# One decoder step on one core: a pool of 52 slots of 576 columns in place of 53 of 568, and another order of the last operations

## The chip, the core and the metric

The kernel runs on one core of a Trainium2 chip. A core has five engines with instruction streams of their own: TensorE (PE in the profile; its weight loads are listed apart as PEld), VectorE (DVE), ScalarE (ACT), GpSimd (POOL) and SyncE (SP), which here only issues transfers. They work on SBUF, a memory of 128 partitions, and TensorE writes its products to PSUM banks of 128 x 512 fp32. Sixteen DMA engines move data between DRAM and SBUF. [...] The metric is the time of one execution on the device, in microseconds, lower being better.

## The reference

A decoder layer is run once for two groups of tokens: a prompt of 512 and 8 samples of 4, together 544 tokens of 1,024 features, all in fp32.

```python
h = rmsnorm(x, norm_mix_pre);  x_r, q, k, v, g = split(h @ w_in)
A = rg_lru(causal_conv4(x_r))                  # gated linear recurrence
B = window_attention(q, k, v)                  # 8 heads, 2 kv heads, window 128, sinks, bias
m = (sigmoid(g_A) * (A @ w_lru_o) + sigmoid(g_B) * (B @ w_attn_o)) @ w_out
x = x + rmsnorm(m, norm_mix_post)
u = causal_conv3(rmsnorm(x, norm_ffn_pre) @ w_up)       # 1024 -> 8192 columns
val, gate = split(u)
x = x + rmsnorm((gelu(gate) * val) @ w_down, norm_ffn_post)   # 4096 -> 1024
```

Returned are `x` of both groups and the states that a next step needs: the end of the recurrence, the last rows ahead of each convolution (among them `s_ffn_conv`, the last two rows of `u` per sample), and the last keys and values.

## The kernel before

**Number format.** Every large product is made of three: weight and activation are each split into a high part of reduced precision and a low rest, and `wh*xh`, `wh*xl` and `wl*xh` are summed in PSUM (`mm`, L165; `product`, L1531). ScalarE makes the high part of a weight by a copy and VectorE the low part by a subtraction (L168). The tokens stand along the columns in two halves, 272 each in the up projection, 256 and 288 in the down projection (`HALF`). A matmul has a weight block of 128 x 128 and a moving operand, the high or low part of an activation tile, of 256 to 288 columns.

**Stages.** In-projection, recurrence, attention, their two projections and the out-projection come first; the feed-forward part starts near 500 us. The up projection handles 32 pairs of a value block and a gate block. A pair is made of seven products of half size instead of eight (`pair`, L1644): `a11`, `a12`, `p2`, `p3`, `p1`, `p4`, `a22`, on the activation tiles `b11`, `b21`, `t2`, `t3`, `t1`, `b22`, `t4` (high parts end in H, low parts in L). They go to PSUM banks called `pux`, `puy` and `puz`. The weights of `p2` and `p4` are sums of blocks that the DMA engines add up in place (`raw_up_s`, L1468 and L1469; those of the last pair are loaded plainly at L1435). After a pair come the convolution taps and the gated product: `z` is the product, `fH` its high part (ScalarE) and `fL = z - fH` (VectorE, L168). Four such blocks make a chunk of the down projection, whose results (`pmdn`) VectorE adds to `ft`, the sum for each of the eight feature blocks (L174). The last chunk is called `dl`.

**Order.** TensorE's order is a table (`plan`) that interleaves the products of up and down projection. One entry is a slot: `slot()` runs what was put down for it (`result`, `later`), splits weights four entries ahead (`consumed`, `ahead`) and lets side jobs go on (`start_at`). The code of the feed-forward part runs under a manual schedule for ScalarE and VectorE, so that these execute in the order in which the code issues; the transfers of SP fall under it from L1987 on, and are placed by the scheduler before. A side job that matters here is `ffn_states` (L1765): three times it transposes a group of state rows into a slot, `ffn_rows_s`, and GpSimd issues four stores of it to DRAM (L1773). The second is started three slots after the `a22` of pair 27.

**Pools.** Most large tiles are slots of one pool, `S`, of 53 buffers of 128 x 568 fp32 (L144): the activation parts, `fH` and `fL`, `ft`, `ffn_rows_s`, the last `raw_up_s` halves, and the last weights. A few tiles of the same width stand outside of the pool. A new tile gets the buffer of a tile that is done with; the first instruction that writes the new tile then waits for the last ones that used the old. A column is 4 bytes, so that a slot is 2,272 bytes per partition. Smaller tiles (`T`, `RAW`, weight parts) come from pools of their own, and `pvn` is a small table of 24 columns with norm weights.

**The end.** Two of the four tiles of 128 prompt tokens are computed with tokens along the partitions (`tokens`, L1921; the last quarter in `ends`, L1952). `tokens_done` (L1932) adds the sum so far (`fr`), has ScalarE square it, and multiplies by the norm's weights (`fg`, the gain): on GpSimd for the first half of the first tile (L1943), else on VectorE (L171). `rstd` makes the tile's norm factor, and `tokens_out` (L1974) applies it, adds `x` in one operation (`stt`, L177) and returns the store of 256 KB. The other tokens, feature-major, are finished by `finish_b` (L1827): per block an `stt` on VectorE and an addition on GpSimd (L1837); `y_blocks` (L1852) then transposes pieces into `yb_p`, which leaves in sixteen small stores on SP (L1866), and into `yb_s`, the samples, which leave in four stores on GpSimd (L1850). `rows_t` (L1870) makes the rest of them on TensorE (`yo`).

Of the kernel before, what the change touches and what calls it, by code (L numbers as in the profile page):

```python
# [11 lines left out]
F32 = mybir.dt.float32  # L12
F32R = mybir.dt.float32r
AF = mybir.ActivationFunctionType
ALU = mybir.AluOpType
AX = mybir.AxisListType

P = 128
# [21 lines left out]
SCALE = HD ** -0.5  # L40
SKEY = 2 * WIN + NKV * NS

S_BUFS = 53
W_BUFS = 12
T_BUFS = 10
RAW_BUFS = 5
SLOT = 568
CH = 4
CHAIN = 10
AHEAD = 4  # L50
# [73 lines left out]
def hawk_step(ctx, tc, I, O):  # L124
    nc = tc.nc
    act, dve, pool, pe = nc.scalar, nc.vector, nc.gpsimd, nc.tensor

    keep = ctx.enter_context(tc.tile_pool(name="const", bufs=1))
    sp = ctx.enter_context(tc.tile_pool(name="slots", bufs=S_BUFS))
    wp = ctx.enter_context(tc.tile_pool(name="wsplit", bufs=W_BUFS))  # L130
# [12 lines left out]
    def S(name, dt=F32):  # L143
        return sp.tile([P, SLOT], dt, tag="s", name=name)  # L144

    def T(name, dt=F32):
        return tp.tile([P, FLAT + 4], dt, tag="t", name=name)

    def RAW(name):
        return rp.tile([P, D], F32, tag="raw", name=name)  # L150

    def PM(name):
        return psm.tile([P, 512], F32, tag="mm", name=name)
# [4 lines left out]
    def SM(name, shape, tag="sm"):  # L158
        return smp.tile(shape, F32, tag=tag, name=name)

    def f32(ap):
        return ap.bitcast(F32)

    def mm(out, l, r, start, stop):
        pe.matmul(out, l, r, start=start, stop=stop)  # L165

    def sub(out, a, b):
        dve.tensor_tensor(out=out, in0=a, in1=b, op=ALU.subtract)  # L168

    def mul(out, a, b):  # L170
        dve.tensor_tensor(out=out, in0=a, in1=b, op=ALU.mult)  # L171

    def add(out, a, b):
        dve.tensor_tensor(out=out, in0=a, in1=b, op=ALU.add)  # L174

    def stt(out, a, s_, b, op0, op1):
        dve.scalar_tensor_tensor(out=out, in0=a, scalar=s_, in1=b, op0=op0, op1=op1)  # L177
# [117 lines left out]
    class Full:  # L295
# [5 lines left out]
        def alloc(self, k):  # L301
            new = S if k or self.name not in APART else (lambda nm, dt: cp.tile([P, SLOT], dt, name=nm))
            self.t[k] = (new(f"{self.name}H{k}", F32R), new(f"{self.name}L{k}", F32R))
            return self.t[k]
# [95 lines left out]
    for r, nme in ((8, "norm_mix_post"), (16, "norm_ffn_pre"), (24, "norm_ffn_post")):  # L400
        nc.sync.dma_start(out=rows_a[r:r + 8, :], in_=I[nme].rearrange("o (k p) -> (o k) p", p=P))
    pv = keep.tile([P, 96], F32, name="pv")
    pvn = keep.tile([P, 24], F32, name="pvn")

    pw = PM("ps_warm")
    ps0 = PX("ps_rows_a0")
# [11 lines left out]
    def newton_rstd(r, v, s_, sq):  # L418

        act.activation(r, sq, AF.Abs_reciprocal_sqrt, scale=1.0 / D, bias=epst)  # L420
        dve.tensor_scalar(v, sq, 1.0 / D, EPS, ALU.mult, ALU.add)
        mul(s_, r, r)
        stt(s_, s_, -0.5, v, ALU.mult, ALU.mult)
        stt(r, s_, 1.5, r, ALU.add, ALU.mult)
# [552 lines left out]
    def gates(c):  # L977
        xH, xL = T(f"xcH{c}", F32R), T(f"xcL{c}", F32R)
        act.activation(xH[:, 0:FLAT], xc[c][:, 0:FLAT], AF.Copy)
        sub(xL[:, 0:FLAT], xc[c][:, 0:FLAT], f32(xH[:, 0:FLAT]))  # L980
        rg[c] = cp.tile([P, SLOT], F32, name=f"rg{c}") if c < RG_APART else S(f"rg{c}")
        yield
# [612 lines left out]
    def slot(k=1, lag=1, limit=10 ** 6, chain_first=False):  # L1595

        for f in todo.pop(turn[0], []):
            f()
        if k and not chain_first:
            consumed(k, lag, limit)  # L1600
        turn[0] += 1
        round_()
        if k and chain_first:
            consumed(k, lag, limit)
# [157 lines left out]
    def by_block(ap):  # L1762
        return ap.rearrange("p (c a d) -> p c a d", a=4, d=32)
# [38 lines left out]
    for i, x in enumerate(plan):  # L1802
# [8 lines left out]
        else:  # L1811
            _, q, c, a = x
# [28 lines left out]
                    if z >= 0:  # L1841
                        y_blocks(z)

    yb = {}

    def samples_out():
        src = yb["s"][:, 0:256].rearrange("p (c d) -> p c d", c=8)
# [4 lines left out]
    def y_blocks(c):  # L1852

        if c == 0:
            yb["p"], yb["s"] = T("yb_p"), T("yb_s")
        dve.transpose(yb["s"][:, 32 * c:32 * c + 32], ft[c][:, SEQ:NT])
        if c > 3:
            return
        o = yb["p"][:, 0:512].rearrange("p (b c d) -> p c b d", b=4, c=4)
        dve.transpose(o[:, c], ft[c][:, 2 * P:3 * P].rearrange("p (b q) -> p b q", b=4))  # L1860
        if c == 3:
            dst = yp[2 * P:3 * P, 0:512].rearrange("(b q) (c a d) -> a b q c d", b=4, a=4, d=32)
            src = yb["p"][:, 0:512].rearrange("p (b c d) -> p b c d", b=4, c=4)
            for a in range(4):
                for b in range(4):
                    nc.sync.dma_start(out=dst[a, b], in_=src[32 * a:32 * a + 32, b])  # L1866

    yo_ = {}

# [40 lines left out]
    def turned():  # L1910
        px = PX("pfo")
        for j in range(4):
            pe.transpose(px[:, j * P:(j + 1) * P], ft[4 + j][:, 0:P], ident)
        row = T("frow0_1")[:, 0:512]
        frow[0, 1] = by_block(row)
        later(1, act.copy, row, px)
# [4 lines left out]
    def tokens(i, kk):  # L1921
        ps = PM(f"ptok{i}_{kk}")
        t = slice(i * P, (i + 1) * P)
        for k in range(CH):
            wh, wl = (usplit["dl", k, kk][j].rearrange("p k n -> p (k n)") for j in range(2))
            fh, fl = (F.t[QL * CH + k][j][:, t] for j in range(2))
            mm(ps, fh, wh, k == 0, False)
            mm(ps, fl, wh, False, False)
            mm(ps, fh, wl, False, k == CH - 1)
        return ps  # L1930

    def tokens_done(i, kk, ps):  # L1932

        fr = T(f"fr{i}_{kk}")[:, 0:512]
        add(by_block(fr), frow[i, kk], by_block(ps[:, 0:512]))
        jk = T(f"jk{i}_{kk}")[:, 0:512]
        act.activation(jk, fr, AF.Square, accum_out=ssq[:, i, kk:kk + 1])
        fg = fgs[i, kk] = T(f"fg{i}_{kk}")[:, 0:512]
        g = gpost[:, kk * 512:(kk + 1) * 512]
        if i or kk:  # L1940
            mul(fg, fr, g)
        else:
            pool.tensor_tensor(out=fg, in0=fr, in1=g, op=ALU.mult)  # L1943

    def rstd(i):
        add(ssq[:, i, 0:1], ssq[:, i, 0:1], ssq[:, i, 1:2])
        st = SM(f"nst_t{i}", [P, 3], "nst_t")
        v, r, s_ = (st[:, z:z + 1] for z in range(3))
        newton_rstd(r, v, s_, ssq[:, i, 0:1])
        return r  # L1950
# [23 lines left out]
    def tokens_out(i, r, z):  # L1974
        o = fgs[i, z]
        stt(o, o, r, xtok[i, z], ALU.mult, ALU.add)
        return lambda: nc.sync.dma_start(out=yp[i * P:(i + 1) * P, z * 512:(z + 1) * 512], in_=o)

    acc = T("acc31")
    gpost = RAW("gpost")  # L1980
# [15 lines left out]
    for _, q, c, a in held:  # L1996
        down(q, c, a, down_done(q, c))
        slot(0)
    for i, kk in ((0, 0), (0, 1), (1, 0)):
        ps = tokens(i, kk)  # L2000
        if (i, kk) == (0, 0):
            slot(0)
            turned()
        slot(0)
        tokens_done(i, kk, ps)
        if (i, kk) == (0, 1):
            r0 = rstd(0)
    while todo or side:
        slot(0)
    samples_out()  # L2010
    outs = [tokens_out(0, r0, z) for z in range(2)]
    for f in outs:
        f()
    fgs[1, 1] = T("fg1_1")[:, 0:512]
    st = SM("nst_t1", [P, 5], "nst_t1")
    v, r, s_, b_, h_ = (st[:, z:z + 1] for z in range(5))
# [53 lines left out]
```

## Time and profile before

| | |
|---|---|
| time, median of 3 runs | 971.44 us (970.93 to 971.70) |
| the profiled execution's own time | 971.33 us |
| its span in the trace | 969.5 us |
| mean granted clock of TensorE | 0.998 of full speed |
| instructions | 20,081 |
| TensorE busy | 99% of the span, 7,598 matmuls |
| VectorE, ScalarE, GpSimd busy | 79%, 57%, 17% |
| read from and written to DRAM | 118.21 MB and 16.74 MB |

The trace covers the span; the 1.8 us between span and time lie around it. Rows of a group give the line of the code, the engine, the operation, `out<-in` with the shape, the count, and behind the bar the busy time in microseconds and the mean of one in nanoseconds; a row of a timeline gives the start and the duration in microseconds. In the table by windows the columns are the stretch and its length, the busy time (and number) of PE, PEld, DVE, ACT and POOL, the granted clock, the share of the time in which the DMA engines had work, and GB/s. "SPq" or "POOLq" is the queue in which an engine waits to issue a transfer. In a list of waits each row names who waited, for what, and the sum, number and longest of the waits.

### The profile page before, as it was taken

The numbers are of one execution on the slowest core, as the hardware profiler recorded it, in microseconds if no ns is written. First come the engines' busy times: TensorE is split into PE (matmuls) and PEld (weight loads), VectorE is DVE, ScalarE is ACT, GpSimd is POOL, SyncE is SP. The second block draws the span as 40 slices with busy tenths as digits, with TensorE's granted clock in tenths as the row PEclk, the third lists the DMA queues.
The fourth block names the chain that finished last, engine by engine and source line by source line (L and its number), as shares of the span: only waits on it lengthen the run. The fifth ranks groups of instructions, "written<-read, shape, count | busy, mean of one in ns | idle before, by whom it ended". The sixth has DMA issues, their size and how long they took to land.

```text
span 969.5 us, 20081 instructions
## 1 busy us (share of the span) xinstructions
PE 959.9 (99%) x7598; PEld 952.4 (98%) x7598; DVE 762.1 (79%) x1625; ACT 550.2 (57%) x1342; POOL 168.5 (17%) x284
## 2 busy tenths in 40 slices
PE   9999999999999999999999999999999999999997
PEld 8999999999999999999999999999999999999996
DVE  5778888857858555689967878887888888888886
ACT  6544443467476425566867665555556565656642
POOL 2142000003406231230011110101011111111024
PEclk9999999999999999999999999999999999999999
DMA  7765536533334537235147575767667685859542
GB/s 226 237 212 185 148 90 155 158 94 88 93 103 152 172 101 197 66 123 178 46 108 196 133 187 141 182 155 170 167 153 196 142 201 134 204 130 234 178 147 93
DMA packets 247596, 147.26 MB, mean 152 GB/s; under 512 B 36324, under 2 KB 231788, under 8 KB 247468
## 3 DMA queue, kind: packets, MB, share of 16 engines
q1 hardware_dynamic: 237468, 124.15, 43.5%
q0 software_dynamic: 9824, 19.55, 11.9%
q10 hardware_dynamic: 208, 2.30, 0.6%
q8 instruction: 59, 0.97, 0.4%
q14 instruction: 37, 0.30, 0.1%
HBM read 118.21 MB, written 16.74 MB: 139 GB/s over the span
## 4 chain that ended last, share of the span: by engine, by line
PE 91%; DVE 5%; ACT 1%; issue 1%; SPq 1%; DMA 1%; DVEq 0%; POOL 0%; ACTq 0%; POOLq 0%
PE pmin L165 20%; PE pmdn L165 17%; PE pux L1531 16%; PE puy L1531 8%; PE pq L1531 6%; PE pmlo L165 5%; PE pmao L165 5%; PE pmout L165 4%; PE puz L1531 4%; PE pg L165 1%; PE pvp L165 1%; PE psc L165 1%; SPq L1866 1%; DVE wl_e L168 1%; DMA pt<-pd 0%
## 5 line engine op out<-in xcount | busy, mean ns | idle before, releaser
L165 PE MATMUL pmin<-hH,wh_in 128*128 128x256 f32 (+1 forms) x568 | 163.9, 291 | 0.0
L165 PE MATMUL pmin<-hL,wh_in 128*128 128x256 f32 (+1 forms) x568 | 162.4, 288 | 0.0
L165 PE MATMUL pmin<-hH,wl_in 128*128 128x256 f32 (+1 forms) x568 | 159.1, 288 | 0.0
L165 PE MATMUL pmdn<-fH,wh_dn 128*128 128x256 f32 (+1 forms) x448 | 129.2, 288 | 0.0
L165 PE MATMUL pmdn<-fH,wl_dn 128*128 128x256 f32 (+1 forms) x448 | 128.8, 287 | 0.0
L165 PE MATMUL pmdn<-fL,wh_dn 128*128 128x256 f32 (+1 forms) x448 | 128.7, 287 | 0.0
L165 PEld LDWEIGHTS pmin<-hH,wh_in 128*128 128x128 f32 x568 | 107.2, 189 | 1.4 <-issue 1.2
L165 PEld LDWEIGHTS pmin<-hL,wh_in 128*128 128x128 f32 x568 | 107.2, 189 | 0.1
L165 PEld LDWEIGHTS pmin<-hH,wl_in 128*128 128x128 f32 x568 | 104.7, 188 | 0.2 <-issue 0.2
L177 DVE SCALAR_TENSOR_TENSOR uc<-u,fv,uc 128x560 f32<-128x560 f32 x128 | 102.0, 797 | 1.7 <-ACT uc L1562 1.2
L165 PEld LDWEIGHTS pmdn<-fH,wl_dn 128*128 128x128 f32 x448 | 84.4, 188 | 0.0
L165 PEld LDWEIGHTS pmdn<-fL,wh_dn 128*128 128x128 f32 x448 | 84.3, 188 | 0.1
L165 PEld LDWEIGHTS pmdn<-fH,wh_dn 128*128 128x128 f32 x448 | 84.2, 188 | 0.1
L1659 ACT COPY u<-pux 128x272 f32<-128x272 f32 x52 | 20.1, 387 | 87.2 <-PE pux L1531 87.2
L168 DVE TENSOR_TENSOR u<-puy,u 128x240 f32<-128x240 f32 (+2 forms) x78 | 24.6, 344 | 48.1 <-PE puy L1531 30.5
L174 DVE TENSOR_TENSOR ft<-ft,pmdn 128x256 f32<-128x256 f32 (+1 forms) x104 | 45.0, 434 | 16.5 <-PE pmdn L165 16.3
L283 ACT ACTIVATE wh_in<-raw_in 128x512 fp32r<-128x512 f32 x70 | 42.2, 624 | 19.2 <-issue 12.0
L290 DVE TENSOR_TENSOR wl_in<-raw_in,wh_in 128x512 fp32r<-128x512 f32 x70 | 47.8, 693 | 1.0 <-ACT wh_in L283 1.0
L1562 ACT ACTIVATE uc<-u,fv 128x560 f32<-128x560 f32 x64 | 48.2, 756 | 0.0
L781 ACT ACTIVATE s<-s,st 128x256 f32<-128x256 f32 (+1 forms) x32 | 15.2, 475 | 53.6 <-DVE st L778 45.9
L168 DVE TENSOR_TENSOR wl_dn<-raw_dn,wh_dn 128x512 fp32r<-128x512 f32 x56 | 38.3, 684 | 3.1 <-ACT wh_dn L1480 3.1
L1469 POOL DMA_DIRECT2D raw_up_s<-raw_up_s x26 | 22.4, 861 | 92.2 <-DMA raw_up_s<-raw_up__11280 5.4
(746 smaller groups left out, 3371.9 us busy)
## 6 DMA issues: line engine op xcount, KB each, us to landing
raw_in<-in_w_in_dram SPq DMA_DIRECT2D x35, 512.0 KB
raw_dn<-in_w_down_dram SPq DMA_DIRECT2D x56, 256.0 KB
raw_up_s<-in_w_up_dram SPq DMA_DIRECT2D x25, 512.0 KB
raw_up_s<-raw_up_s POOLq DMA_DIRECT2D x26, 256.0 KB, 4.2
raw_ao<-in_w_attn_o_dram SPq DMA_DIRECT2D x8, 512.0 KB
raw_lo<-in_w_lru_o_dram SPq DMA_DIRECT2D x8, 512.0 KB
raw_out<-in_w_out_dram SPq DMA_DIRECT2D x8, 512.0 KB
pd<-pb SPq DMA_DIRECT2D x12, 256.0 KB
```

What stands on the lines that cost most here:

```text
L165: pe.matmul(out, l, r, start=start, stop=stop)
L168: dve.tensor_tensor(out=out, in0=a, in1=b, op=ALU.subtract)
L174: dve.tensor_tensor(out=out, in0=a, in1=b, op=ALU.add)
L177: dve.scalar_tensor_tensor(out=out, in0=a, scalar=s_, in1=b, op0=op0, op1=op1)
L283: act.activation(hl[0], raw, AF.Copy)
L290: (eng or dve).tensor_tensor(out=hl[1], in0=raw, in1=f32(hl[0]), op=ALU.subtract)
L781: act.activation(s3[:, j, :], s3[:, j, :], AF.Exp, bias=ng[:, j:j + 1], accum_out=sm[:, j:j + 1])
L1469: pool.dma_start(out=w["p4"], in_=w["p2"], accum_op=ALU.add)
L1531: pe.matmul(ps[:, :HN], w, x, start=start and k == 0 and i == 0, stop=stop and k == 3 and i == 2, skip_group_check=True)
L1562: act.activation(yt[j][:, 0:FLATU], u[:, 0:FLATU], AF.Copy, scale=fv[:, j:j + 1])
L1659: act.copy(e[nm_], z)
L1866: nc.sync.dma_start(out=dst[a, b], in_=src[32 * a:32 * a + 32, b])
```

## The change

The slots become 576 columns wide, 2,304 bytes, and there are 52 of them; `pvn` is allocated with 32 columns. These two make every tile begin at a multiple of 64 bytes. At the end, `tokens_done` returns the gain as a function that the caller runs; both gains of the first token tile run on VectorE, one behind the other, and its two `stt` and stores come before VectorE's next steps for the second tile and the samples. The sixteen small stores of `yb_p` become a list that is sent in three parts, around these two stores.

```diff
-S_BUFS = 53
+S_BUFS = 52
-SLOT = 568
+SLOT = 576
...
-    pvn = keep.tile([P, 24], F32, name="pvn")
+    pvn = keep.tile([P, 32], F32, name="pvn")[:, 0:24]
...
-    yb = {}
+    yb, pieces = {}, []
...
             for a in range(4):
                 for b in range(4):
-                    nc.sync.dma_start(out=dst[a, b], in_=src[32 * a:32 * a + 32, b])
+                    pieces.append(lambda a=a, b=b: nc.sync.dma_start(out=dst[a, b], in_=src[32 * a:32 * a + 32, b]))
+            send(10)
+
+    def send(n):
+        for f in pieces[:n]:
+            f()
+        del pieces[:n]
...
         fg = fgs[i, kk] = T(f"fg{i}_{kk}")[:, 0:512]
-        g = gpost[:, kk * 512:(kk + 1) * 512]
-        if i or kk:
-            mul(fg, fr, g)
-        else:
-            pool.tensor_tensor(out=fg, in0=fr, in1=g, op=ALU.mult)
+        return lambda: mul(fg, fr, gpost[:, kk * 512:(kk + 1) * 512])
...
-    for i, kk in ((0, 0), (0, 1), (1, 0)):
+    gains = []
+    for i, kk in ((0, 0), (0, 1)):
         ps = tokens(i, kk)
-        if (i, kk) == (0, 0):
+        if not kk:
             slot(0)
             turned()
         slot(0)
-        tokens_done(i, kk, ps)
-        if (i, kk) == (0, 1):
-            r0 = rstd(0)
+        gains.append(tokens_done(i, kk, ps))
+    for f in gains:
+        f()
+    r0 = rstd(0)
+    ps = tokens(1, 0)
+    tokens_out(0, r0, 0)()
+    send(3)
+    gain = tokens_done(1, 0, ps)
+    tokens_out(0, r0, 1)()
+    send(len(pieces))
     while todo or side:
         slot(0)
     samples_out()
-    outs = [tokens_out(0, r0, z) for z in range(2)]
-    for f in outs:
-        f()
+    gain()
```

Fewer slots mean that a tile takes over another buffer than before, and its first writer waits for others. On VectorE, in the up projection while pair 28 is handled, this stands in the stream now; in brackets are the semaphores that an instruction waits for (DMASW are transfers issued by GpSimd, DMAHW those by SP and ScalarE; `wl_s_a` and `wl_s_p` are low parts of weights):

```order
 L168 TENSOR_TENSOR wl_s_a_12438<-raw_up__12140,wh_s_a_12437 128x512 [waits DVE_49,Activation_49]
 L168 TENSOR_TENSOR u_12416<-puy_12334,u_28_12347 128x272 [waits PE_49]
-L168 TENSOR_TENSOR fL_12459<-z_12371,fH_12458 128x544 [waits DVE_49,Activation_49]
+L168 TENSOR_TENSOR fL_12459<-z_12371,fH_12458 128x544 [waits DMASW4_49,DMASW5_49,DMASW0_49,DMASW6_49,DVE_49,Activation_49]
 L168 TENSOR_TENSOR wl_s_p_12462<-raw_up_s,wh_s_p_12461 128x512 [waits DMASW3_49,DVE_49,Activation_49]
 L174 TENSOR_TENSOR ft_7725<-ft_7725,pmdn_7_1_12465 128x288 [waits PE_49]
```

The order stays; `fL` of block 27 now waits for four transfers issued by GpSimd, which are the stores of the second `ffn_rows_s`.

On SP, some entries further in the code, the two plain loads for the last pair (L1435) stand among the other weight loads:

```order
 L1444 DMA raw_up__12433<-in_w_up_dram 128x8x128 [waits DMAHW3_49,DVE_49]
 L1444 DMA raw_up_s<-in_w_up_dram 128x8x128 [waits DMAHW5_49,DVE_49]
-L1435 DMA raw_up_s_12611<-in_w_up_dram 128x4x128 [waits DMASW5_49,DMASW4_49,DMASW6_49,DMASW0_49,PE_49]
+L1435 DMA raw_up_s_12611<-in_w_up_dram 128x4x128 [waits PE_49]
 L1435 DMA raw_up_s_12612<-in_w_up_dram 128x4x128 [waits DMAHW6_49,PE_49]
 L1444 DMA raw_dn_2_12506<-in_w_down_dram 128x4x128 [waits DMAHW7_49,DMAHW0_49,DVE_49]
```

The wait for these four stores has left the load.

At the end, on VectorE, the operations for the first token tile (`fg_0_13513`, `fg_1_13550`), for the samples (`yb_s`) and for the first half of the second tile (`fr_0_13578`, `fg_0_13582`) stand like this now:

```order
+L177 SCALAR_TENSOR_TENSOR fg_0_13513<-fg_0_13513,nst_t_13554,xtok_13258 128x512
+L174 TENSOR_TENSOR fr_0_13578<-frows,ptok_0_13560 128x512
+L177 SCALAR_TENSOR_TENSOR fg_1_13550<-fg_1_13550,nst_t_13554,xtok_13258 128x512
 L1856 STREAM_TRANSPOSE yb_s<-ft_7387 128x32
 L1856 STREAM_TRANSPOSE yb_s<-ft_7493 128x32
 L1856 STREAM_TRANSPOSE yb_s<-ft_7623 128x32
 L1856 STREAM_TRANSPOSE yb_s<-ft_7725 128x32
-L174 TENSOR_TENSOR fr_0_13583<-frows,ptok_0_13566 128x512
-L171 TENSOR_TENSOR fg_0_13587<-fr_0_13583,gpost 128x512
-L177 SCALAR_TENSOR_TENSOR fg_0_13513<-fg_0_13513,nst_t_13560,xtok_13258 128x512
-L177 SCALAR_TENSOR_TENSOR fg_1_13557<-fg_1_13557,nst_t_13560,xtok_13258 128x512
+L171 TENSOR_TENSOR fg_0_13582<-fr_0_13578,gpost 128x512
```

The two `stt` of the first tile and the addition of the second have moved ahead of the four transposes. Further up, the gain of `fg_0_13513` has come to VectorE from GpSimd, ahead of that of `fg_1_13550`. On SP the stores were, at the end of the program,

```order
-L1866 DMA out_dram<-yb_p 32x4x32 x16
-L1977 DMA out_dram<-fg_0_13513 128x512
-L1977 DMA out_dram<-fg_1_13557 128x512
-L1881 DMA out_dram<-yo_13637 128x512 x2
-L1977 DMA out_dram<-fg_0_13587 128x512
-L1977 DMA out_dram<-fg_1_13597 128x512
```

and are now

```order
+L1866 DMA out_dram<-yb_p 32x4x32 x10
+L1979 DMA out_dram<-fg_0_13513 128x512
+L1866 DMA out_dram<-yb_p 32x4x32 x3
+L1979 DMA out_dram<-fg_1_13550 128x512
+L1866 DMA out_dram<-yb_p 32x4x32 x3
+L1887 DMA out_dram<-yo_13637 128x512 x2
+L1979 DMA out_dram<-fg_0_13582 128x512
+L1979 DMA out_dram<-fg_1_13597 128x512
```

Their number and sizes are the same; the first tile's two stand inside the small ones.

## The prediction

> **What bounds the kernel now.** I read the page first (its busy shares and the chain that ended last), then who TensorE waited for, then the stretches of the span, and last the timelines of the two places where the change alters a wait.
>
> ```profile
> span 969.5 us, 20081 instructions
> PE 959.9 (99%) x7598; PEld 952.4 (98%) x7598; DVE 762.1 (79%) x1625; ACT 550.2 (57%) x1342; POOL 168.5 (17%) x284
> PE 91%; DVE 5%; ACT 1%; issue 1%; SPq 1%; DMA 1%; DVEq 0%; POOL 0%; ACTq 0%; POOLq 0%
> ...
> PE pmdn L165 <- DVE wl_dl L168: 0.2, 1, 0.2
> ...
> 500.00:930.00 430.00, 430.00 (x3429) 430.00 (x3428) 360.44 (x725) 258.86 (x639) 48.15 (x58) 1.00 0.68 168
> ...
> 961.40:969.50 8.10, 1.19 (x11) 0.95 (x9) 2.82 (x9) 2.10 (x6) 0.98 (x2) 0.77 0.70 245
> ```
>
> TensorE works 959.9 of 969.5 us, at full clock (1.00 from 500 to 930 us), and is never idle for 430 us on end; its last wait for another engine, at the end of the down projection, is 0.2 us. So until 961.4 the time is the sum of the steps between matmuls, and another engine counts only where it becomes later than TensorE's need. After 961.4 TensorE has next to nothing left; 8.1 us follow that belong to the last operations and the stores. The change has three terms: the place of the operands (A), a wait that moves because the pool has one slot less (B), and the order at the end (C).
>
> **A: operands at multiples of 64 bytes.** A slot of 568 columns is 2,272 bytes, 35.5 times 64, so that every second slot starts 32 bytes past a multiple. By the addresses that the slots get, 3,138 of the moving operands start so; afterwards none does. In the up projection the products of t1 and t3 read tiles that all lie 32 past; in those of t4 and b22 the high parts, which two thirds of the matmuls read, lie on the multiple.
>
> ```profile
> L1531 PE MATMUL puy<-t3H,wh_s_p 128*128 128x272 f32 x104 | 30.3, 292 | 0.0
> L1531 PE MATMUL puy<-t3H,wl_s_p 128*128 128x272 f32 x104 | 30.1, 290 | 0.0
> L1531 PE MATMUL puy<-t3L,wh_s_p 128*128 128x272 f32 x104 | 29.7, 286 | 0.0
> L1531 PE MATMUL pux<-b22H,wh_s_p 128*128 128x272 f32 x104 | 29.9, 287 | 0.0
> L1531 PE MATMUL pux<-b22H,wl_s_p 128*128 128x272 f32 x104 | 30.0, 289 | 0.0
> L1531 PE MATMUL pux<-b22L,wh_s_p 128*128 128x272 f32 x104 | 30.0, 288 | 0.0
> ...
> 883.14 0.29 PE L1531 MATMUL puy<-t3H,wh_s_p 128*128 128x272 f32 x1
> 884.65 0.28 PE L165 MATMUL pmdn<-fH,wh_dn 128*128 128x256 f32 x1
> 889.17 0.29 PE L1531 MATMUL pux<-b22H,wh_s_p 128*128 128x272 f32 x1
> 890.67 0.29 PE L1531 MATMUL puy<-t4H,wh_s_a 128*128 128x272 f32 x1
> ```
>
> The three groups of t3 sum to 90.1 us, those of b22 to 89.9: 0.2 us over 312 matmuls, 0.6 ns of each. A product of twelve steps takes 884.65 - 883.14 = 1.51 us for t3 and 890.67 - 889.17 = 1.50 us for b22, which is the resolution of the rows. So a matmul gains between 0 and 0.6 ns: 0 to 1.9 us over 3,138. I take the middle, 0.3 ns, **-1.0 us**. A loss is not excluded: 2,304 bytes are nine times 256, so that afterwards all slots start at the same place within 256 bytes, which the trace of before cannot show; I allow 0.3 ns the other way, +1.0 us, as the bound.
>
> [...]
>
> **B: 52 slots.** Most slots are free long before they are taken again. I compared, for each wait that is new, when its releaser ends in the trace with when the waiting instruction starts. They are apart by microseconds except in two places. One, the low part of block 19, comes 0.1 us behind a matmul and costs VectorE that much at most. The other is `fL` of block 27. It now takes the slot of `ffn_rows_s`, whose four stores to DRAM are issued by GpSimd; before, the load of the last `raw_up_s` halves, on SP, took that slot and bore the wait.
>
> ```profile
> SPq L1435 <- DMA out_dram<-ffn_rows_s: 4.4, 1, 4.4
> ...
> 875.15 0.95 POOL L1773 DMA_DIRECT2D out_dram<-ffn_rows_s  x1
> ...
> 880.77 0.92 SPq L1435 DMA_DIRECT2D raw_up_s<-in_w_up_dram  x2
> ...
> 877.59 0.71 DVE L168 TENSOR_TENSOR fL<-z,fH 128x544 fp32r<-128x544 f32 x1
> 878.23 0.69 DVE L168 TENSOR_TENSOR wl_s_p<-raw_up_s,wh_s_p 128x512 fp32r<-128x512 f32 x1
> ...
> 879.91 0.68 DVE L168 TENSOR_TENSOR wl_s_p<-p,wh_s_p 128x512 fp32r<-128x512 f32 x1
> ...
> 883.64 0.68 DVE L168 TENSOR_TENSOR wl_s_p<-raw_up__12199,wh_s_p 128x512 fp32r<-128x512 f32 x1
> ...
> 881.89 0.28 PE L1531 MATMUL pux<-t2H,wl_s_p 128*128 128x272 f32 x1
> ...
> 883.39 0.29 PE L1531 MATMUL puy<-t3H,wl_s_p 128*128 128x272 f32 x1
> ...
> 886.32 0.29 PE L1531 MATMUL pux<-t1H,wl_s_p 128*128 128x272 f32 x1
> ```
>
> SP stood 4.4 us for the last of these stores and went on at 880.77, so it landed by then. VectorE started `fL` at 877.59; now it stands there until 880.77, **3.18 us**, and all that is queued behind it on VectorE is late by as much, for it has no pause up to the third `wl_s_p`. These low weights are what TensorE waits for. The first ends at 878.92 and is read at 881.89, a slack of 2.97; the second ends at 880.59, read at 883.39, slack 2.80; the third ends at 884.32, read at 886.32, slack 2.00. What 3.18 leaves over is 0.21, 0.38 and 1.18 us. TensorE's delays do not add up (the later ones contain the earlier), so the term is the largest, **+1.2 us**, and TensorE has no gap behind it in which it could be made up. Bounds: 0 if the store lands 2 us sooner; if it lands later, each microsecond counts in full. SP is freed by the same step and issues its two 256 KB loads some 3 us earlier, into a full queue:
>
> ```profile
> 878.00:880.00 2.00, 2.00 (x17) 2.00 (x17) 2.00 (x5) 2.00 (x6) 0.00 (x0) 1.00 1.07 267
> ```
>
> At 267 GB/s these 0.52 MB take 2.0 us; if the store were to stand behind all of it, B would be 3.2 us.
>
> **C: the end.** The first token tile's gain moves from GpSimd to VectorE, its two `stt` move ahead of the transposes of the samples, and its two stores go between the sixteen small ones of `yb_p`.
>
> ```profile
> 961.73 0.86 SPq L1977 DMA_DIRECT2D out_dram<-fg  x2
> 962.68 0.88 SPq L1881 DMA_DIRECT2D out_dram<-yo  x2
> ...
> 963.79 1.84 SPq L1977 DMA_DIRECT2D out_dram<-fg  x2
> ...
> 964.00:965.00 1.00, 0.00 (x0) 0.00 (x0) 0.43 (x1) 0.00 (x0) 0.00 (x0) 1.00 1.04 399
> ...
> 966.00:967.00 1.00, 0.00 (x0) 0.00 (x0) 0.00 (x0) 0.00 (x0) 0.00 (x0) 0.50 1.06 406
> 967.00:968.00 1.00, 0.00 (x0) 0.00 (x0) 0.00 (x0) 0.00 (x0) 0.00 (x0) 0.50 0.63 242
> ...
> 954.60 1.29 POOL L1943 TENSOR_TENSOR fg<-fr,gpost 128x512 f32<-128x512 f32 x1
> 955.86 2.00 POOL L1837 TENSOR_TENSOR ft<-ft,x1r 128x288 f32<-128x288 f32 x2
> 960.07 2.31 POOL L1850 DMA_DIRECT2D out_dram<-yb_s  x4 [2.21 <-DVE fg L171]
> ...
> 956.39 0.73 DVE L174 TENSOR_TENSOR ssq<-ssq 128x1 f32<-128x1 f32 x1
> 961.20 0.15 DVE L174 TENSOR_TENSOR nst_t<-ssq 128x1 f32<-128x1 f32 x1
> ```
>
> Seven stores of 256 KB leave from 961.73 on, and from 964 the DMA engines are full at some 400 GB/s until past 967.5, two microseconds after the last issue ends. The end is a backlog. Two stores less in it are 0.52 MB, at 400 GB/s 1.3 us, the upper bound. But the stream of the other five begins with `yo` at 962.68, 0.95 us after the stream of before, and nothing issues it sooner: 1.3 - 0.95 = 0.35 us if it ramps up as slowly as the old one, nearly the whole 1.3 if it starts at full rate. In the middle, 0.8. Against it: GpSimd's four `yb_s` stores were released by VectorE at 960.07, after the gain of the second tile; the transposes that they need now come 1.4 us later (two `stt`, L177), so their 4 x 32 KB fall into the backlog, 0.3 us at 400 GB/s. I take **-0.5 us**; the bound below is +0.5, from the lock that the rivals speak of. VectorE has the 0.8 us of a gain more to do, but GpSimd's pair at 955.86 moves up to 954.6, and what it held up becomes shorter (`ssq`, 0.73 us against 0.15 for the same operation at 961.20).
>
> **Sum.** -1.0 + 1.2 - 0.5 = -0.3 us. The profiled execution took 971.33 us, 1.8 more than its span, 0.11 below the median of 971.44. So 971.0 as a profile, **971.1 us** as a median: no difference that can be told, since about 0.2%, 1.9 us, is what a measurement of this kernel can tell from none (faster is below 969.5, slower above 973.4).
>
> **Rivals.** (1) *The wait at block 27 stays hidden and the places pay in full.* The other three `ffn_rows_s` stores were issued 3 to 5 us earlier, and if the last one lands 2 us sooner B is 0.2. With A at its end of 1.9 and C at 1.2: -2.9, 968.5 us. For it: the groups of t3; against it: SP's 4.4 us. Chance 0.18. (2) *VectorE waits longer than SP did*, because the freed loads are in front of the store: B 3.2, the rest as above, +1.7, 973.1 us, slower. It decides as soon as the store lands after 881.3 (3.7 us of wait, 1.7 of them on TensorE, against the 1.5 that A and C bring). For it: DMA share 1.07 at that time; against it: the queue was that full before, without these loads. Chance 0.16, and in half of it the time passes 973.4. (3) *The places buy nothing*, the change not doing what its words say: A is 0, +0.7, 972.1 us. For it: 1.51 against 1.50 us per product. Chance 0.18. (4) *GpSimd's adds block the moved gain.* In before, `ssq` has two inputs in SBUF and ran 0.73 us beside GpSimd's adds and 0.15 us without them. The moved gain also has two such inputs and would stand at 955.6 until GpSimd's last add ends at some 956.6 (954.60 + 2.00), so that all of VectorE's tail is 0.7 us later, SP waits for the first store and the whole stream moves by 0.5: C is +0.3, the sum +0.5, 971.9 us. Chance 0.14.
>
> [...]
>
> **How the numbers follow.** The forecast has 0.34; with (3) and (4), 971 to 972.1, two thirds, all within 0.2%. Most of (1), 0.16, and 0.02 of the forecast are faster by more: **0.18**. Half of (2) and 0.04 of the combinations of (2) with (3) and (4) are slower by more: **0.12**. Same: **0.70**. The forecast's own range is 970 to 972.2. To leave out no more than 2 in 10 the range reaches to 969.0, into (1), and to 973.2, past the middle of (2).
>
> **What would show it.** A: the groups of t3 at 89.9 us instead of 90.1, and the step of a product unchanged to 0.01 us. B: VectorE's list of waits names `fL` behind the store of `ffn_rows_s` with about 3 us, SP's 4.4 us are gone, and TensorE shows 1.2 us of idle time before `wl_s_p` between 881 and 888. C: the stores `fg` of the first tile at some 959 and 961, DMA share below 1 by 967.2, and `yb_s` issued after 961.3. Wrong would be: idle time of TensorE anywhere else, a step of the matmuls that differs by over 0.02 us per product, or stores that end as late after TensorE's last matmul as before, 8.2 us to the end of the span.

## The result, and the profile after

The changed kernel takes 977.22 us (median of 6; 975.0 to 979.51) where the kernel before takes 971.37 us: 1.0058 times as long, with an interval of 1.0048 to 1.0068. That is 5.9 us, slower, and outside of the range of the prediction. Its executions also lie apart as those of the kernel before never do, and in step with TensorE's mean granted clock: 975.0 and 975.2 us at 0.998, 977.1 to 977.9 at 0.996, 979.5 at 0.994. The profiled execution took 975.24 us, so it shows the lower end of this; what the others add has to come from experiments.

The page of the changed kernel (its span, and the busy time of the queue that SP fills, as a share of 16 engines' span), then its list of waits for TensorE and one row of that for VectorE:

```profile
span 973.4 us, 20081 instructions
...
q1 hardware_dynamic: 237468, 124.15, 45.8%
...
PE pux L1531 <- DVE wl_s_p L168: 1.5, 2, 1.1
...
PE pq L1531 <- DVE b11L L168: 0.4, 1, 0.4
...
DVE fL L168 <- DMA out_dram<-ffn_rows_s: 4.1, 1, 4.1
```

In the page of the kernel before the same queue reads

```profile
q1 hardware_dynamic: 237468, 124.15, 43.5%
```

The wait of `fL` is where the prediction put it, and TensorE waits for `wl_s_p` as foreseen, but longer. Something that the prediction had not thought of stands in the two lines of `q1`: the same packets and the same bytes took some 5% more time of the DMA engines. (The 0.4 us for `b11L`, near 420 us, is another wait that fewer slots bring.) The timeline of the changed kernel around block 27:

```profile
875.59 0.95 POOL L1773 DMA_DIRECT2D out_dram<-ffn_rows_s  x1
...
876.34 0.47 SPq L1444 DMA_DIRECT2D raw_up_s<-in_w_up_dram  x1
877.95 1.35 SPq L1435 DMA_DIRECT2D raw_up_s<-in_w_up_dram  x2
...
877.69 0.44 DVE L168 TENSOR_TENSOR u<-puy,u 128x272 f32<-128x272 f32 x1 [1.38 <-PE puy L1531]
882.18 0.72 DVE L168 TENSOR_TENSOR fL<-z,fH 128x544 fp32r<-128x544 f32 x1 [4.05 <-DMA out_dram<-ffn_rows_s]
...
883.57 0.39 PE L1531 MATMUL pux<-t2H,wl_s_p 128*128 128x272 f32 x1 [1.09 <-DVE wl_s_p L168]
...
888.83 0.39 PE L1531 MATMUL pux<-t1H,wl_s_p 128*128 128x272 f32 x1 [0.39 <-DVE wl_s_p L168]
...
891.78 0.35 PE L1531 MATMUL pux<-b22H,wh_s_p 128*128 128x272 f32 x1
```

The store lands for VectorE at 882.18 and not at 880.77. The operation ahead, `u`, started at 877.24 in the kernel before and at 877.69 here, so TensorE's and VectorE's stream came 0.45 us late into this place. `b22H` started at 889.17 before and at 891.78 here, 2.61 us late: block 27 costs TensorE **2.16 us**, more than the sum's +1.2 and inside the bounds of B.

The end of both kernels: the last matmuls, the samples' stores of GpSimd and, for the changed kernel, SP's stores and the DMA engines by stretches. First the kernel before:

```profile
961.12 1.47 PE L1878 MATMUL pyo<-ident,ft 128*128 128x128 f32 x12
...
964.00:966.00 2.00, 0.00 (x0) 0.00 (x0) 0.43 (x1) 0.00 (x0) 0.00 (x0) 0.95 1.03 398
966.00:968.00 2.00, 0.00 (x0) 0.00 (x0) 0.00 (x0) 0.00 (x0) 0.00 (x0) 0.50 0.85 324
```

and after the change:

```profile
963.48 1.47 PE L1884 MATMUL pyo<-ident,ft 128*128 128x128 f32 x12
...
964.63 2.31 POOL L1850 DMA_DIRECT2D out_dram<-yb_s  x4 [5.98 <-DVE fg L171]
...
961.59 0.35 SPq L1979 DMA_DIRECT2D out_dram<-fg  x1
...
963.50 0.38 SPq L1979 DMA_DIRECT2D out_dram<-fg  x1
...
966.38 2.07 SPq L1979 DMA_DIRECT2D out_dram<-fg  x2
...
966.00:968.00 2.00, 0.00 (x0) 0.00 (x0) 0.79 (x2) 0.00 (x0) 0.94 (x2) 1.00 0.87 223
968.00:970.00 2.00, 0.00 (x0) 0.00 (x0) 0.00 (x0) 0.00 (x0) 0.00 (x0) 1.00 1.03 288
970.00:972.00 2.00, 0.00 (x0) 0.00 (x0) 0.00 (x0) 0.00 (x0) 0.00 (x0) 0.53 0.54 203
```

From the end of TensorE's last matmul to the end of the span it was 969.5 - 962.6 = 6.9 us; now it is 973.4 - 964.95 = 8.5 us. The first tile's two stores do leave earlier against TensorE's work, 1.9 us ahead of and just at its last group instead of 0.6 us behind its start, and yet the end is longer by **1.5 us**. The samples' stores, issued at 960.07 before, now leave at 964.63, and full engines (1.03) move 288 GB/s where they moved 398.

So the profiled execution's 3.9 us are 0.45 + 2.16 + 1.5, less some 0.25 that TensorE wins back between block 27 and its end (891.78 - 889.17 = 2.61 us late at `b22H`, 963.48 - 961.12 = 2.36 at the last group).

### The profile page after: what moved, and what is told of

Read it like the earlier page. It is cut to its first block, busy times and chain, and to the rows that moved or that the text cites. A ratio compares the mean times of both kernels' runs of the same rounds, so it can differ in the third digit from the quotient of the medians.

```text
span 973.4 us, 20081 instructions
## 1 busy us (share of the span) xinstructions
PE 960.6 (99%) x7598; PEld 952.2 (98%) x7598; DVE 761.6 (78%) x1626; ACT 550.4 (57%) x1342; POOL 166.4 (17%) x283
## 3 DMA queue, kind: packets, MB, share of 16 engines
q1 hardware_dynamic: 237468, 124.15, 45.8%
## 4 chain that ended last, share of the span: by engine, by line
PE 88%; DVE 6%; DMA 2%; ACT 1%; issue 1%; SPq 0%; POOL 0%; POOLq 0%; DVEq 0%; ACTq 0%
PE pmin L165 20%; PE pmdn L165 17%; PE pux L1531 15%; PE puy L1531 8%; PE pq L1531 6%; PE pmlo L165 5%; PE pmao L165 5%; PE pmout L165 4%; PE puz L1531 4%; PE pg L165 1%; PE pvp L165 1%; PE psc L165 1%; DMA out_dram<-ffn_rows_s 1%; DVE wl_e L168 1%; DMA x<-in_x_prompt_dram 1%
## 5 line engine op out<-in xcount | busy, mean ns | idle before, releaser
L781 ACT ACTIVATE s<-s,st 128x256 f32<-128x256 f32 (+1 forms) x32 | 15.2, 475 | 55.4 <-DVE st L778 43.3
```

Of the source, the lines that this page charges most:

```text
L781: act.activation(s3[:, j, :], s3[:, j, :], AF.Exp, bias=ng[:, j:j + 1], accum_out=sm[:, j:j + 1])
```

## Experiments

Each was timed against the kernel before, five or more executions each; the kernel before stood between 971.27 and 971.37 us in all of them. The theory at the start, S: a wait at block 27 that stalls TensorE and lets its clock fall, and an end made longer by the samples' stores.

**The parts apart.** The slots alone:

```diff
-S_BUFS = 53
+S_BUFS = 52
-SLOT = 568
+SLOT = 576
-    pvn = keep.tile([P, 24], F32, name="pvn")
+    pvn = keep.tile([P, 32], F32, name="pvn")[:, 0:24]
```

> The kernel before with 52 slots of 576 columns and the wider pvn, the old end. Theory S (the stall at block 27 does the harm, in two ways: TensorE waits about 2.2 us there, and the pause can make the granted clock fall for a while in some executions): best executions at about 973.7 us (971.4 + 2.2 for the wait, 0.4 at the start, -0.3 for the steps), the others 2 to 4 us above it with a mean clock of 0.996 or 0.994. Rival A (the place of the slots does it: all at the same place within 256 bytes, and the clock falls for that): the same spread. Rival C (all of it comes from the end of the program): 971.4 and no spread.

Measured: 976.87 us (973.34 to 977.54), ratio 1.0051 (1.0037 to 1.0064), clocks 0.996 to 0.998, the lowest time at the highest clock. The new end alone (the change's diff without these lines):

> The kernel before, 53 slots of 568, with the new end alone. Theory S with its part for the end (about 1.3 us, because stores of 128-byte pieces now stand inside the stream of the large stores): 972.7 us, clock 0.998 in every execution, no spread. As predicted at first: 970.9. Rival C: 973.5 to 977 with the spread.

Measured: 971.95 us (971.27 to 972.24), ratio 1.0006 (0.9997 to 1.0015), and no lower clock. By the times alone that can't be told from none, but its profile shows the same TensorE timeline as before and 970.3 - 962.6 = 7.7 us behind the last matmul instead of 6.9:

```profile
span 970.3 us, 20080 instructions
...
961.14 1.47 PE L1884 MATMUL pyo<-ident,ft 128*128 128x128 f32 x12
```

One slot less, with the columns left alone:

```diff
-S_BUFS = 53
+S_BUFS = 52
```

> The kernel before with 52 slots of the old 568 columns: the same new wait at block 27, the places of the operands as scattered as before, the old end. Theory S: 973.6 us in the best executions and lower clocks (0.994 to 0.996, 976 to 978 us) in some of the others. Rival A: no lower clock, 973.6 us in all, or 971.4 if the places make the wait as well.

Measured: 978.27 us (977.31 to 979.71), ratio 1.0071 (1.0058 to 1.0083), clocks 0.995 to 0.998. So having 52 slots does the main harm with either width (in both kernels the smaller pools behind the slots have moved as well, which matters further down), and this profile has the lower clock in it. Its wait of VectorE, and its stretches around the stall:

```profile
DVE fL L168 <- DMA out_dram<-ffn_rows_s: 6.4, 1, 6.4
...
882.00:884.00 2.00, 0.69 (x6) 0.47 (x4) 0.00 (x0) 0.63 (x1) 0.00 (x0) 1.00 1.13 322
884.00:886.00 2.00, 0.00 (x0) 0.00 (x0) 1.33 (x3) 0.00 (x0) 0.00 (x0) 0.82 0.18 54
886.00:888.00 2.00, 1.95 (x8) 1.95 (x9) 2.00 (x4) 0.00 (x0) 0.00 (x0) 0.50 0.00 0
888.00:890.00 2.00, 2.00 (x11) 2.00 (x10) 2.00 (x6) 0.92 (x2) 0.00 (x0) 0.50 0.00 0
890.00:892.00 2.00, 2.00 (x11) 2.00 (x10) 2.00 (x4) 0.00 (x0) 0.00 (x0) 0.50 0.44 131
892.00:894.00 2.00, 2.00 (x18) 2.00 (x17) 1.95 (x4) 1.29 (x2) 0.86 (x1) 0.97 0.12 14
```

TensorE stands from 882.7 to 886 us; near the end of the pause its clock goes to 0.50 and stays there until 892: 11 matmuls in 2 us instead of 18. VectorE waits 6.4 us, not 4.1.

**The wait taken away.** In the changed kernel, the stores are issued two pairs earlier, so that they have landed when `fL` comes:

```diff
-        for g0, g1, p_ in ((0, 2, 19), (2, 3, 27)):
+        for g0, g1, p_ in ((0, 2, 19), (2, 3, 25)):
```

> The changed kernel with the second transposition and stores of state rows started after pair 25 and not 27, so that the stores have long landed when fL of block 27 takes their slot. Theory S: no wait of VectorE there, none of TensorE, clock 0.998 in all executions, 972.8 us (971.4 + 1.3 for the end, 0.4 - 0.3). Rival A: the wait is gone but the lower clocks stay: 972.8 in the best, up to 977 in others.

Measured: 972.63 us (971.94 to 973.86), ratio 1.0016 (1.0007 to 1.0025), clocks 0.997 or 0.998. The wait and the lower clocks go together, 4.6 of the 5.9 us. What stays is the end:

```profile
span 970.8 us, 20081 instructions
...
960.89 1.47 PE L1884 MATMUL pyo<-ident,ft 128*128 128x128 f32 x12
```

TensorE is done at 962.4 us, 0.2 us sooner than before the change; 8.4 us follow.

**Is it the pause?** The kernel before, pools and end untouched, with VectorE made late at the same place by writing the same `fL` several times:

```diff
-            sub(fl[:, 0:NT], zt[p_][:, 0:NT], f32(fh[:, 0:NT]))
+            for _ in range(6 if p_ == 27 else 1):       # 11 in the second kernel
+                sub(fl[:, 0:NT], zt[p_][:, 0:NT], f32(fh[:, 0:NT]))
```

> The kernel before, pools and end as they were, with fL of block 27 written six times instead of once (the same values): VectorE is 5 x 0.64 = 3.2 us late there and nothing else changes. If the slack rows of the prediction are right (2.97, 2.80 and 2.00 us), TensorE loses 1.2 us and the clock stays: 972.5 us, 0.998. If a short pause is enough for the clock to fall: 974 us or more in some executions.

> As the former with eleven writes: VectorE 6.4 us late. By the slacks TensorE stands 3.4 us before the first of the three products and up to 4.4 us in all. Theory K (a pause of over 3 us lowers the granted clock for some 3.4 us or twice that, as in the profiles with the long wait): 976 to 978 us with clocks of 0.995 to 0.997. Rival (the lower clock belongs to the change of the pool and not to the pause): 975.8 us at 0.998 in every execution.

Measured: 973.18 us (972.93 to 973.69), ratio 1.0020 (1.0011 to 1.0029), clock 0.998 or more in every execution; and 978.35 us (977.57 to 979.17), ratio 1.0073 (1.0061 to 1.0086), clocks 0.995 to 0.997. The second one's timeline and stretches:

```profile
877.57 8.30 DVE L168 TENSOR_TENSOR fL<-z,fH 128x544 fp32r<-128x544 f32 x11
...
882.00:884.00 2.00, 0.02 (x1) 0.00 (x0) 1.90 (x4) 0.00 (x0) 0.00 (x0) 1.00 0.86 250
884.00:886.00 2.00, 0.00 (x0) 0.00 (x0) 1.93 (x4) 0.00 (x0) 0.00 (x0) 0.56 0.04 12
886.00:888.00 2.00, 1.47 (x6) 1.47 (x7) 2.00 (x4) 0.00 (x0) 0.00 (x0) 0.50 0.00 0
888.00:890.00 2.00, 2.00 (x11) 2.00 (x10) 2.00 (x5) 0.80 (x2) 0.00 (x0) 0.50 0.00 0
```

One more write costs (8.30 - 0.71) / 10 = 0.76 us, not the 0.64 that was assumed, so VectorE was 3.8 and 7.6 us late. The slacks of the prediction then give 3.8 - 2.0 = 1.8 us for the first: 1.9 were measured. For the second they give 5.6 us, and 7.0 were measured. In its profile block 27 costs TensorE 6.8 us (`b22H` against `u`, as above), so that 1.2 us of the rest fall in the stretch with the half clock, behind a pause of 4.5 us. Here the clock fell in a pause of 4.5 us without any change of pool; in the profile of the first, whose longest pause is 0.7 us, it stays at 1.00.

**Why the store lands so late.** First idea: the two loads that the change frees on SP stand in front of it. They are put some entries further back, with their slots taken as before:

```diff
-            for z, raw in enumerate(raws[key]):
-                nc.sync.dma_start(out=raw, in_=w_up[...])
+            def behind(raw2):
+                for z, raw in enumerate(raw2):
+                    nc.sync.dma_start(out=raw, in_=w_up[...])
+                yield
+            start_at(now[0] + 1, behind(raws[key]))
```

> The changed kernel with the two plain loads of the last pair issued some entries later on SP, behind the next loads; their slots are taken as before. Theory L (these loads, freed by the change, stand in front of the fourth store of the state rows and make it land 2 to 3 us later): it lands some 5 us after its issue, VectorE waits 3 us, TensorE 1.2 us, the clock stays at 0.998 in nearly all executions, and the time is 974 us. Rival (the store is slow for another reason, such as the place of its rows): the wait of VectorE stays between 4 and 6.5 us, with lower clocks and 975 to 978 us.

Measured: 977.14 us (975.5 to 979.75), ratio 1.0059 (1.0047 to 1.0072), clocks 0.995 to 0.997. The idea falls: no load is issued between 876.65 and 889.09, and VectorE waits 6.3 us (the first row, a wait for another load, is needed further down):

```profile
867.33 0.69 DVE L174 TENSOR_TENSOR p<-raw_up_s,raw_up__12199 128x512 f32<-128x512 f32 x1 [1.22 <-DMA raw_up_s<-in_w_up_dram]
...
876.65 0.37 SPq L1448 DMA_DIRECT2D raw_up_s<-in_w_up_dram  x1
889.09 0.37 SPq L1448 DMA_DIRECT2D raw_dn<-in_w_down_dram  x1
...
DVE fL L168 <- DMA out_dram<-ffn_rows_s: 6.3, 1, 6.3
```

Second idea, from the lines of `q1`: the place of the tiles. Behind the slots in SBUF lie the smaller pools, among them `RAW`, where weights are loaded, and `T`, from which the last stores leave. By the addresses of the built programs, these two start at multiples of 256 bytes in the kernel before; 52 slots of 2,304 bytes and the wider `pvn` move them to 64 bytes short of one (still a multiple of 64, which a few tiles of single columns are not), 52 slots of 568 columns to 32 past one. Both kernels were shifted by `pvn` alone, the changed one on to the next multiple of 256, the one before to 64 past one:

```diff
-    pvn = keep.tile([P, 32], F32, name="pvn")[:, 0:24]      # changed kernel
+    pvn = keep.tile([P, 48], F32, name="pvn")[:, 0:24]
...
-    pvn = keep.tile([P, 24], F32, name="pvn")               # kernel before
+    pvn = keep.tile([P, 40], F32, name="pvn")[:, 0:24]
```

> The changed kernel as it is, but pvn with 48 columns, so that all later tiles start at multiples of 256. The wait at block 27 is there as in the changed kernel. Theory M2 (slow transfers at places 64 past a multiple of 128 make a load, and with it the stores of the state rows, 1 to 1.5 us later; that turns a stall of TensorE of 1 to 2 us into one of 3.5 us, which lowers the clock): quick packets (27.8 ns) bring the median from 977.2 to about 974.5 us, with fewer of the lower clocks. Rival (the store lands late at any rate, its landing varies by 2 us of itself): the median stays at 976 to 977.5 us, packets of 27.8 ns or not.

> The kernel before, 53 slots of 568 columns and the old end, with pvn allocated 64 bytes longer, so that the pools behind the slots (weights as loaded, small tiles) start 64 past a multiple of 128 as they do in the changed kernel. No wait changes. Theory M (the place makes the transfers slow): the packets of SP's queue take 5% more time, the part after TensorE's last matmul grows from 6.95 to about 7.35 us, and the time from 971.3 to 971.7 us. Rival N (slow transfers come from 52 slots or from 576 columns): packet time, end and time as before, 971.3 us.

Measured: 973.71 us (973.2 to 975.56), ratio 1.0027 (1.0016 to 1.0037), for the changed kernel, 3.5 us less than without the 64 bytes, and no clock below 0.997. And 971.88 us (971.4 to 972.42), ratio 1.0006 (0.9997 to 1.0015), for the kernel before, which the times alone can't tell from none. The `q1` line of the first:

```profile
q1 hardware_dynamic: 237468, 124.15, 43.3%
```

and of the second, with one row of its VectorE, the issue of the fourth store and the wait of SP for it:

```profile
q1 hardware_dynamic: 237468, 124.15, 45.5%
...
866.45 0.69 DVE L174 TENSOR_TENSOR p<-raw_up_s,raw_up__12199 128x512 f32<-128x512 f32 x1 [1.09 <-DMA raw_up_s<-in_w_up_dram]
...
876.37 0.95 POOL L1773 DMA_DIRECT2D out_dram<-ffn_rows_s  x1
...
SPq L1435 <- DMA out_dram<-ffn_rows_s: 7.5, 1, 7.5
```

In the kernel before the same operation had no pause ahead of it:

```profile
865.28 0.69 DVE L174 TENSOR_TENSOR p<-raw_up_s,raw_up__12199 128x512 f32<-128x512 f32 x1
```

Nothing was changed but a start by 64 bytes, and SP's packets take 45.5% instead of 43.5%; when the changed kernel is moved on to a multiple of 256, they go back to 43.3%. In the shifted kernel before a load of `raw_up_s` lands 1.1 us too late for `p`; what hangs on `p`, the additions and the stores of GpSimd, is 1.2 us later (the fourth store is issued at 876.37 and not at 875.15); and SP waits 7.5 us for the store instead of 4.4. Of these 3.1 us the late issue explains 1.2. The rest is not shown to come from the place: from its issue until SP went on the store took 7.5 us here and 5.6 in the kernel before, but 7.6 with the samples first (further down), where the places are the old ones. In this kernel the late store itself holds up only SP, and another late load costs TensorE 0.5 us (`b22H` starts at 889.71 instead of 889.17). In the changed kernel it is VectorE that waits for the store.

The late load also divides the profiles at hand. In the three in which 52 slots come with the lower clock, `p` waits for it, 1.30 us with the slots alone, 1.11 with one slot less and 1.22 with the loads behind; in those of the changed kernel and of its shift, with the clock at 1.00, it does not. None of the six profiles with 53 slots at the old places has it. With the state rows early it comes at either place (1.78 and 0.69 us), so that the place is not all of it.

The same 64 bytes, with the state rows early:

```diff
-    pvn = keep.tile([P, 32], F32, name="pvn")[:, 0:24]
+    pvn = keep.tile([P, 48], F32, name="pvn")[:, 0:24]
...
-        for g0, g1, p_ in ((0, 2, 19), (2, 3, 27)):
+        for g0, g1, p_ in ((0, 2, 19), (2, 3, 25)):
```

> The changed kernel with the state rows early, and pvn allocated with 48 columns instead of 32: nothing else changes but that every later tile starts 64 bytes further on, at a multiple of 256 and no longer 64 past a multiple of 128. Theory M (transfers are quick where the SBUF side starts at a multiple of 128, as the smaller pools did in the kernel before; 64 past it they are slow): the mean packet of 512 bytes returns from 29.4 to 27.8 ns, the part after TensorE's last matmul from 8.4 to 7.7 us, and the time from 972.6 to 971.8 us. Rival N (the place does not matter, and the end is long for another reason): 29.4 ns, 8.4 us, 972.6 us.

Measured: 972.74 us (971.38 to 973.51), ratio 1.0011 (1.0002 to 1.0020): no better than without the 64 bytes, although packets and end are as theory M has them:

```profile
span 970.9 us, 20081 instructions
...
q1 hardware_dynamic: 237468, 124.15, 43.4%
...
961.85 1.47 PE L1884 MATMUL pyo<-ident,ft 128*128 128x128 f32 x12
```

7.6 us follow the last matmul instead of 8.4; but TensorE reaches it at 961.85 where it was at 960.89. The slots, too, now start at multiples of 256, and TensorE's steps are longer, most of all between 430 and 490 us: from start to start the matmuls of 272 columns take 125.26 ns on average instead of 124.96, 1.1 us over 3,524. Why was not found out.

**The end.** With 53 slots of 568 and the new end, the samples' transposes and stores go ahead of the first tile's last operations:

```diff
     ps = tokens(1, 0)
+    while todo or side:
+        slot(0)
+    samples_out()
     tokens_out(0, r0, 0)()
...
-    while todo or side:
-        slot(0)
-    samples_out()
     gain()
```

> 53 slots of 568 columns and the new end, with the transposes and the stores of the samples ahead of the first tile's two last operations instead of behind them. Theory T (the end is 0.7 us longer because the samples' stores fall into the stream of the large ones): the part after TensorE's last matmul goes from 7.65 back to about 6.9 us, 971.2 us. Rival U (the six small stores that now stand behind the large ones make it longer): 7.6 us and 971.9 us as with the samples late.

Measured: 970.95 us (970.52 to 971.54), ratio 0.9995 (0.9986 to 1.0004), 1.0 us less than the new end alone. Its samples' stores, last matmuls and DMA engines:

```profile
span 969.2 us, 20080 instructions
...
960.23 2.31 POOL L1850 DMA_DIRECT2D out_dram<-yb_s  x4 [3.94 <-DVE fr L174]
...
961.21 1.47 PE L1884 MATMUL pyo<-ident,ft 128*128 128x128 f32 x12
...
964.00:966.00 2.00, 0.00 (x0) 0.00 (x0) 0.52 (x1) 0.00 (x0) 0.00 (x0) 1.00 0.92 353
966.00:968.00 2.00, 0.00 (x0) 0.00 (x0) 0.00 (x0) 0.00 (x0) 0.00 (x0) 0.89 0.79 302
```

6.5 us follow the last matmul: 0.4 less than before the change, 1.2 less than with the samples late. GpSimd taking the last six small stores as well:

```diff
-    send(3)
...
-    send(len(pieces))
...
+    send(6, pool)           # right ahead of samples_out()
     samples_out()
```

> As with the samples first, and the last six of the sixteen small stores issued by GpSimd, so that SP has the first tile's two stores directly behind ten small ones. Theory T: 0.3 us less than with the samples first alone, 970.9 us, since the large stores begin at about 959 and 960 us and nothing small stands between them. Rival U: 971.0 us, less by the whole 0.7. Against both: GpSimd's additions of the last two blocks are held up by its stores and TensorE's last transposes wait for them: 971.5 us or more.

Measured: 970.92 us (970.87 to 971.41), ratio 0.9996 (0.9987 to 1.0005), so no more than the samples first. The small stores of `yb_p` on SP were not what held the end.

These two are the best versions found; against the kernel before their 0.4 us can't be told from nothing by the times.

## Why the prediction was wrong

**The frame** held: TensorE's chain up to 961 us, and three terms. The sign did not, because of two sizes and two mechanisms that it lacked.

**A** had looked at TensorE's moving operands alone. There the sum was small, as said, but by luck: it is made of larger changes of both signs. With the state rows early, where no pause stretches a matmul, the groups of `t3` sum to 89.4 us instead of 90.1, 0.7 better; those of `b22` to 90.1, 0.2 worse. From start to start, over all rows of the traces before and of that run, matmuls of 272 columns became 0.45 ns shorter (3,524 of them, -1.6 us), those of 288 columns 1.1 ns shorter (1,811, -2.0 us) and those of 256 columns 1.6 ns longer (1,821, +2.9 us), -0.7 us in all, between the -1.0 taken and the rival that the places buy nothing. With the 0.4 us for `b11L` against it, TensorE ended 0.2 us sooner. That a width can lose was not among the terms, and why it does was not found out. The step that failed is the one that left out who else reads and writes these bytes: the transfers. Their packets got some 5% slower (45.8% where it was 43.5%), which is neither in the sum nor among the rivals. That the place does it the two shifts by 64 bytes show, 43.5% against 45.5% and 45.8% against 43.3%; by what mechanism they do not show, nor which boundary counts. By the built programs the pool of the down weights starts 128 past a multiple of 256 in both kernels with the quick packets, and in the kernel before the packets of 512 bytes in `q1` took 27.5 ns on average from 500 to 930 us, where these weights are loaded, and 27.9 ns in the first 330 us, where they are not. Multiples of 64 were not enough (45.8% in the changed kernel); multiples of 128 were not tried by themselves.

**B** had the place, the queue and the slacks right. VectorE 4.05 us late with slacks of 2.97 and 2.00 gives 1.1 us and 2.1 us; the profile shows 1.09 and 2.16. Wrong was 880.77 as the landing of the store, read from one execution of the kernel before and carried over unchanged. SP's wait for the same store was 4.4, 5.3, 6.5 and 4.6 us in profiles of four kernels in which that part does not differ (the one before, the new end, the samples first, GpSimd sending), and 7.5 us where only the places moved. As a wait of SP this had next to no price and so looked like a constant. Rival (2) had the sign, the place and its condition (past 881.3), but not the cause: with the freed loads put behind, VectorE waited 6.3 us all the same.

**The clock** is a mechanism that was missing. Pauses of 1.1 us (the changed kernel's profile) and 1.6 us (moved on by 64 bytes) left it at 1.00; pauses of 3.4 to 4.5 us came with a clock of 0.50 for 3.4 us (the slots alone) or 6.8 us (one slot less, the loads behind, eleven writes). So the price of the late store is not linear. Each microsecond beyond the slack of 2.0 counts once up to a point: waits of 4.05 and 4.52 us cost TensorE 2.2 and 2.6 us. Then 0.7 to 1.9 us come on top: waits of 6.49, 6.36 and 6.34 us cost 5.3, 6.3 and 6.4. In three of the four profiles with the lower clock it fell 2.2 to 2.7 us after the pause began, and in that of the slots alone 4.3 us after. The prediction read "clock 1.00" as a property of the stretch, though TensorE's own idle time was one of its terms. None of the changed kernel's slower executions was profiled, so how the 2.0 us of its median above the profiled execution divide into a longer wait and the clock stays open. In the profiles of the slots alone, of one slot less and of the loads behind, block 27 costs 3.1 to 4.2 us more than in the changed kernel's, and 2.3 to 2.4 of these are the longer wait.

**C** was -0.5 with a bound of +0.5; it is +0.8 with the old places and +1.5 with the new ones. The failing term is the samples' stores: 4 x 32 KB priced by their bytes at the rate of the large stores, 0.3 us. Moved out of the backlog again they give back 1.2 us. Once the samples are out of the way, the profile has 0.4 us less behind the last matmul than before the change, near the lower of the two figures given for the two early stores. The slower gain of rival (4) can be seen: VectorE's two gains of the first tile take 1.87 us, of which the first takes 1.27, started at 957.93 while GpSimd's last additions run until 958.65; the other gains with this shape take 0.65 and 0.68 us in the same profile. But SP's first store left 0.1 us after the ten small ones (0.3 with the new end alone), so that it cost little.

## What to carry to other kernels

A pool that gets a slot less moves waits from one engine to another: ask of each moved wait not only when its releaser ended in this trace but how far that end varies, and which engine stands there now; a wait that costs next to nothing on a queue of transfers can cost all of its length beyond the slack on VectorE (here SP's 4.4 us cost next to nothing, VectorE's 4.05 us cost TensorE 2.16). When sizes of tiles are changed "for alignment", look where the pools behind them come to stand: here 64 past, 64 short of and 32 past a multiple of 256 all made the packets of the transfers slower (45.5%, 45.8% and 45.2% instead of 43.5%). And where TensorE is always busy, a pause of 3.4 us and more was dearer than its length, here by 0.7 to 1.9 us.

## What the runs showed of the hardware

- One shift of the smaller pools by 64 bytes, `RAW` and `T` from a multiple of 256 to 64 past one, made SP's packets take 45.5% of the DMA engines' time instead of 43.5%, and came with 7.2 us after the last matmul instead of 6.9 (970.3 - 963.1 us). It left TensorE's steps as they were: up to 866 us the two timelines agree, and the 104 matmuls of `t3H` with `wh_s_p` take 292 ns on average in both.
- TensorE's granted clock fell to 0.50 in four profiles, in pauses of 3.4 to 4.5 us or 0.8 us behind one, and came back 3.4 or 6.8 us later; pauses up to 1.6 us did not move it.
- Four stores of 32 KB, moved with their transposes so that they fall into a full queue, lengthened the end by 1.2 us, four times their share by bytes (0.3 us at the 398 GB/s of 964 to 966 us in the kernel before). Whether the size of their pieces or their queue does it was not tried apart.
